# The roots of three norms by two reciprocals and one product, and the last half row of the output scaled and stored in two pieces

## The chip, the cores and the metric

The kernel runs on one core of a Trainium2 chip, as one program. The metric is the device time of one execution in microseconds (us). Before the change three runs gave 902.17, 900.99 and 902.10 us, with a median of 902.1. The five engines are named as in the profile: TensorE is PE (its weight loads PEld), VectorE is DVE, ScalarE is ACT, GpSimd is POOL, and SyncE (SP) issues most DMAs.

## The reference

One layer (DEPTH is 1) on 1024 tokens of 1024 channels, in float32. The norms are what the change touches: the first and the last have one root for each token, `layernorm` has one too.

```python
def rmsnorm(x, g):
    xf = x.astype(jnp.float32)
    y = xf * lax.rsqrt(jnp.mean(xf * xf, axis=-1, keepdims=True) + EPS)
    return (y * g.astype(jnp.float32)).astype(x.dtype)
...
        h = rmsnorm(x, norm_g[l])
        proj = h @ w_in[l]
        q, k, v, za, u, vs, zs, gm = jnp.split(proj, IN_SPLITS, axis=-1)
        ...
        a = window_sink_attention(q, k, v, att_sinks[l])
        a = (a * jax.nn.silu(za)) @ w_att_out[l]
        sgo = chunked_spatial_gating(jax.nn.gelu(u, approximate=False),
                                     jax.nn.gelu(vs, approximate=False),
                                     sg_w[l], sg_b[l], sg_ln_g[l], sg_ln_b[l])
        sgo = (sgo * jax.nn.silu(zs)) @ w_sg_out[l]
        ga, gs = jnp.split(jax.nn.sigmoid(gm + b_merge[l]), N_BRANCHES, axis=-1)
        y = ga * a + gs * sgo
        x = x + y @ w_o[l]
    return rmsnorm(x, final_g)
```

`chunked_spatial_gating` begins with `layernorm(v, ln_g, ln_b)`, whose root is that of the variance plus EPS (1e-6).

## The kernel before, in words

All large products are made on TensorE by a scheme of seven products for eight: a pair of 512-column halves of an input and of a weight is summed and subtracted into forms (`b11`, `t1`, `t2`, `b21`, `t3`, `b22`, `t4`), and each float32 operand is split into a high part in a rounded format (`wh`, or a form's `h`) and the low rest (`wl`, or a form's `l`). A product is then three matmuls for each 128 rows: high by high, high by low, low by high. ScalarE makes the high part by a cast or copy, VectorE the low part by a subtraction (`split`, lines 164 and 165; `form_of`, lines 642 and 643).

At the start, the eight tiles of `x` (128 tokens each) are loaded, and `scale_of(t)` squares and sums a tile on ScalarE (line 614) and calls `rstd_of`. `turned_half` scales each half of the tile by the root and the gain on VectorE (line 624), and TensorE transposes it, four blocks of 128 x 128 into a `ps_sc` bank (line 629). `form_of` makes `T_b11h`, `T_b21h` on ScalarE and `T_b11l`, `T_b21l` on VectorE out of these banks, and ScalarE copies the banks out for later sums (lines 656 and 658). The first large product starts at once behind, `first_product` (its matmuls are line 750, its copy line 773), tile by tile, between the transposes. Its weights come from HBM and are split by `split_vs` (line 727 makes a `wl` on VectorE). Ahead of all this TensorE runs matmuls on ones (line 554).

`rstd_of` computes one over the root of the mean plus epsilon. Before the change ScalarE makes the root `rt`, VectorE its reciprocal `r0`, and one Newton step in full follows, r0 * (1.5 - 0.5 * ve * r0 * r0), with `ve` the mean plus epsilon on VectorE: five VectorE instructions for one column (lines 137, 141, 144, 151, 152), six for eight columns. With `times_minus_2` the last root of the program ends one instruction earlier (line 146): it is then -2 times the wanted value, and the gains of that row are multiplied by -0.5 ahead of time (`g_last`, line 1942).

At the end, the output projection runs in four pairs of token tiles (`for p in range(4)`). Each quarter of a pair is added to `x` (line 1904), squared and summed on ScalarE (line 1906), and when both halves of a row tile are there, `rstd_of` is called (the first half's sum gives the base). `scale_and_store` scales by root and gain and stores. For the first three pairs this happens inside the next pair, with the stores on the POOL queue. For the last pair (p = 3) two quarters are multiplied by the gain on GpSimd ahead of the root (line 1910) and then by the root on ScalarE (line 1924), the other two are scaled on VectorE (line 1930); the last product is made in two pieces of 256 columns (line 1993), and its sum of squares too (line 1995).

The kernel does not write the engines' order by hand: a scheduler places the instructions of each engine's queue, with its own estimate of times, within the data's order and some order-only links (`after`). Engines run their queues in order and wait for each other by semaphores. The small tiles `st` come from a rotation of 16 buffers, those of eight columns from one of 5.

Of the kernel before, what the change touches and what calls it, by code (L numbers as in the profile page):

```python
# [30 lines left out]
P = 128  # L31
# [21 lines left out]
def hybrid_tile(  # L53
# [52 lines left out]
    nc.gpsimd.memset(eps_sb[:], EPS)  # L106
# [27 lines left out]
    def rstd_of(ss, scale, base=EPS, n=1, times_minus_2=False):  # L134

        ve = mtile([P, n], F32, f"st{n}", 16 if n == 1 else 5)
        of_mean.append(nc.vector.tensor_scalar(ve[:], ss, scale, base, op0=ALU.mult, op1=ALU.add))
        rt = mtile([P, n], F32, f"st{n}", 16 if n == 1 else 5)
        of_root.append(nc.scalar.activation(rt[:], ss, AF.Sqrt, bias=eps_sb[:] if base is EPS else base, scale=scale))
# [3 lines left out]
        if n == 1:  # L143
            nc.vector.scalar_tensor_tensor(e[:], ve[:], r0[:], r0[:], op0=ALU.mult, op1=ALU.mult)
            if times_minus_2:
                nc.vector.scalar_tensor_tensor(e[:], e[:], 3.0, r0[:], op0=ALU.subtract, op1=ALU.mult)
                return e
        else:
            nc.vector.tensor_mul(e[:], ve[:], r0[:])
            nc.vector.tensor_mul(e[:], e[:], r0[:])  # L150
        nc.vector.tensor_scalar(e[:], e[:], -0.5, 1.5, op0=ALU.mult, op1=ALU.add)
        nc.vector.tensor_mul(e[:], e[:], r0[:])
# [92 lines left out]
    def half_of(half):  # L245
        return slice(half * HALF, (half + 1) * HALF)
# [1635 lines left out]
    g_out, g_last = g_both[:, 0:2, :], g_both[:, 2:4, :]  # L1882
# [8 lines left out]
    for p in range(4):  # L1891
# [10 lines left out]
        def add_and_square(i, half, src, sign):  # L1902
# [4 lines left out]
            if p == 3 and i == half:  # L1907
                scaled[i, half] = mtile([P, HALF], F32, gtag(), 1, pool)
                gain = (g_last if i else g_out)[:, half, :]
                nc.gpsimd.tensor_tensor(scaled[i, half][:], z, gain, op=ALU.mult)  # L1910
            if i in sq:
                sq[i] = rstd_of(ss[:], 1.0 / D, sq[i][:])
            else:
                nc.vector.tensor_scalar(ss[:], ss[:], 1.0 / D, EPS, op0=ALU.mult, op1=ALU.add)
                sq[i] = ss

        def scale_and_store(i, p=p, t=t, xr=xr, sq=sq, scaled=scaled):
            r = sq[i]
            row = slice((t + i) * P, (t + i + 1) * P)
            for e in range(2):  # L1920
# [8 lines left out]
                gain = (g_last if p == 3 and i else g_out)[:, e, :]  # L1929
                by_gain = nc.vector.scalar_tensor_tensor(z, z, r[:], gain, op0=ALU.mult, op1=ALU.mult)  # L1930
                if p < 3 or i == 0:

                    after(by_gain, pace[0])
# [6 lines left out]
        copied = nc.scalar.copy(x12[:], acc)  # L1940
        if p == 2:
            after(nc.scalar.mul(g_last, g_out, -0.5), copied)
# [45 lines left out]
        for e in range(2):  # L1988
# [7 lines left out]
            if e == 0:  # L1996
                base = mtile([P, 1], F32, "st1", 16)
                nc.vector.scalar_tensor_tensor(base[:], ss[:], 1.0 / D, sq[1][:], op0=ALU.mult, op1=ALU.add)
            else:
                sq[1] = rstd_of(ss[:], 1.0 / D, base[:], times_minus_2=True)  # L2000
# [85 lines left out]
```

## Time and profile before

| | |
|---|---|
| runs | 902.17, 900.99, 902.10 us |
| the profiled execution | 900.83 us, span 899.0 us |
| PE busy | 890.0 us (99%) |
| DVE busy | 683.5 us (76%) |
| ACT busy | 529.5 us (59%) |
| POOL busy | 153.6 us (17%) |
| granted clock of TensorE | 0.998 (mean) |
| HBM | 147.74 MB read, 86.11 MB written |

The span is the time from the first to the last instruction of the profiled execution; the execution's own time is 1.8 us longer. Rows of the order of time give the start in us from the span's start, the duration in us, the engine, the line, the operation, and out<-in by tile names. "x2" behind a row means that two instructions are merged in it, with the duration from the first one's start to the last one's end. What stands in brackets is the idle time ahead of it and what ended that.

### The profile page before, as it was taken

Reading aid. Unit: us, or ns where it says so; the run is one execution under the profiler, and the core shown is the slowest. Engines: PE = TensorE matmul, PEld = TensorE weight load, DVE = VectorE, ACT = ScalarE, POOL = GpSimd, SP = SyncE. Lnnn points to the kernel's source line nnn. Section 1 sums busy time; section 2 is a strip of 40 time slices with the busy share of each in tenths; the row PEclk is TensorE's granted clock in tenths of the full one; section 3 lists DMA queues with packets and bytes.
Section 4 is the critical chain, followed back from the end, with each engine's and each line's share of the span. In section 5 each row is a group of like instructions: output and inputs, shape, how many; then the busy total and the mean of one; then the engine's idle time right before and its main releaser. Section 6 shows DMA issues by size and latency. Waiting matters only on the chain.

```text
span 899.0 us, 13239 instructions
## 1 busy us (share of the span) xinstructions
PE 890.0 (99%) x4306; PEld 745.2 (83%) x4306; DVE 683.5 (76%) x1248; ACT 529.5 (59%) x1062; POOL 153.6 (17%) x218
## 2 busy tenths in 40 slices
PE   9999999999999999999999999999999999999997
PEld 6888888888888888888888888888888888888885
DVE  7859966666687788888878888647797488479986
ACT  7866533334445567677777776755585376467453
POOL 4322222203030001111210111101121121110012
PEclk9999999999999999999999999999999999999999
DMA  9997888858778767878786789899899789998533
GB/s 331 216 270 205 267 204 174 167 156 263 254 252 281 216 191 213 217 149 209 186 219 227 250 240 202 221 333 361 297 293 370 288 227 258 305 294 287 185 116 119
DMA packets 132750, 213.77 MB, mean 238 GB/s; under 512 B 12777, under 2 KB 61161, under 8 KB 132682
## 3 DMA queue, kind: packets, MB, share of 16 engines
q1 hardware_dynamic: 110072, 149.74, 50.0%
q0 software_dynamic: 22464, 62.93, 31.4%
q8 instruction: 34, 0.56, 0.2%
q14 instruction: 34, 0.28, 0.1%
q10 hardware_dynamic: 146, 0.27, 0.1%
HBM read 147.74 MB, written 86.11 MB: 260 GB/s over the span
## 4 chain that ended last, share of the span: by engine, by line
PE 98%; DVE 1%; ACT 0%; issue 0%; DVEq 0%
PE ps_mm L355 42%; PE ps_o L355 27%; PE ps_tp L355 7%; PE ps_sc L1344 3%; PE ps_sc L355 3%; PE ps_tp L750 2%; PE ps_o L1431 2%; PE ps_o L750 2%; PE ps_tp L1390 2%; PE ps_mm L750 2%; PE ps_tp L1015 2%; PE ps_sc L750 1%; PE ps_sc L629 1%; PE ps_sc L554 1%; DVE wl L727 0%
## 5 line engine op out<-in xcount | busy, mean ns | idle before, releaser
L164 ACT CAST wh<-s 128x1024 fp32r<-128x1024 f32 (+1 forms) x79 | 79.3, 1005 | 91.8 <-PE ps_mm L355 42.0
L165 DVE TENSOR_TENSOR wl<-wr,wh 128x512 fp32r<-128x512 f32 (+1 forms) x77 | 72.0, 937 | 54.1 <-ACT wh L164 53.4
L165 DVE TENSOR_TENSOR wl<-s,wh 128x1024 fp32r<-128x1024 f32 (+1 forms) x79 | 92.9, 1176 | 10.5 <-ACT wh L164 10.4
L164 ACT CAST wh<-wr 128x512 fp32r<-128x512 f32 (+1 forms) x77 | 63.0, 820 | 59.1 <-PE ps_mm L355 30.8
L355 PE MATMUL ps_o<-T_t1h,wh 128*128 128x512 f32 x148 | 58.6, 396 | 0.0
L355 PE MATMUL ps_o<-T_t1h,wl 128*128 128x512 f32 x148 | 57.7, 390 | 0.0
L355 PE MATMUL ps_o<-T_t1l,wh 128*128 128x512 f32 x148 | 57.6, 389 | 0.0
L1359 ACT ACTIVATE pr<-ps_sc,sm 128x192 f32<-128x192 f32 (+2 forms) x128 | 50.9, 410 | 8.3 <-DVE sm L1353 7.3
L355 PE MATMUL ps_mm<-T_t3h,wh 128*128 128x512 f32 x140 | 54.9, 392 | 0.0
L355 PE MATMUL ps_mm<-T_b11h,wh 128*128 128x512 f32 x140 | 54.9, 392 | 0.0
L355 PE MATMUL ps_mm<-T_b11l,wh 128*128 128x512 f32 x140 | 54.7, 391 | 0.0
L355 PE MATMUL ps_mm<-T_t3h,wl 128*128 128x512 f32 x140 | 54.6, 390 | 0.0
L355 PE MATMUL ps_mm<-T_b11h,wl 128*128 128x512 f32 x140 | 54.6, 390 | 0.0
L355 PE MATMUL ps_mm<-T_t2h,wl 128*128 128x512 f32 x140 | 54.6, 390 | 0.0
L355 PE MATMUL ps_mm<-T_t2h,wh 128*128 128x512 f32 x140 | 54.6, 390 | 0.0
L355 PE MATMUL ps_mm<-T_t2l,wh 128*128 128x512 f32 x140 | 54.6, 390 | 0.0
L355 PE MATMUL ps_mm<-T_t3l,wh 128*128 128x512 f32 x140 | 54.5, 389 | 0.0
L355 PE MATMUL ps_mm<-T_t4h,wh 128*128 128x512 f32 x136 | 53.5, 393 | 0.0
L355 PE MATMUL ps_mm<-T_t4h,wl 128*128 128x512 f32 x136 | 53.2, 391 | 0.0
L355 PE MATMUL ps_mm<-T_t4l,wh 128*128 128x512 f32 x136 | 53.0, 389 | 0.0
L309 POOL DMA_DIRECT2D sums<-in_w_dram x40 | 29.4, 930 | 91.8 <-ACT x L373 42.7
L355 PE MATMUL ps_o<-T_b22h,wh 128*128 128x512 f32 x108 | 42.7, 395 | 0.0
(420 smaller groups left out, 2452.0 us busy)
## 6 DMA issues: line engine op xcount, KB each, us to landing
wr<-in_w_dram SPq DMA_DIRECT2D x86, 256.0 KB
sums<-in_w_dram POOLq DMA_DIRECT2D x20, 512.0 KB, 6.5
s<-sums SPq DMA_DIRECT2D x20, 512.0 KB
q_hl<-qhl SPq DMA_DIRECT2D x16, 512.0 KB
q<-q_hl SPq DMA_DIRECT2D x64, 128.0 KB
y_dr<-x POOLq DMA_DIRECT2D x28, 256.0 KB, 7.1
g<-in_w_dram POOLq DMA_DIRECT2D x12, 512.0 KB, 6.5
wr<-in_w_dram SPq DMA_DIRECT2D x11, 512.0 KB
```

Source lines behind the costliest of these rows:

```text
L164: hi_of.append(nc.scalar.copy(hi, src))
L165: return nc.vector.tensor_sub(lo, src, hi.bitcast(F32))
L309: return lambda: paced(nc.gpsimd.dma_start(dst, src, accum_op=op))
L355: nc.tensor.matmul(acc, lt, rt, start=fresh and k == 0 and n == 0, stop=k == 3 and n == 2, skip_group_check=True,)
L554: feed(nc.tensor.matmul(idle[:], ones_r[:, 0:P], ones_r, start=True, stop=True))
L629: turns.append(nc.tensor.transpose(pt[:, i * P : (i + 1) * P], xt[:, k * P : (k + 1) * P], ident[:]))
L750: mm = nc.tensor.matmul(acc[:], lt, rt, start=fresh and k == 0 and n == 0, stop=k == 3 and n == terms[-1], skip_group_check=True,)
L1015: nc.tensor.matmul(pm[:, t * P : (t + 1) * P], xh[:, half * 4 + t, g * P : (g + 1) * P], bias[-1][1][:, g % 4, :], start=True, stop=True,)
L1344: nc.tensor.matmul(sc[:, i, k0:], q_of[:, c, i * P : (i + 1) * P], kt[:, f, k0:], start=f == 0, stop=f == 1,)
L1359: nc.scalar.activation(held_in[c, i], sc[:, i, lo:hi], AF.Exp, bias=nmax[:, c, i : i + 1], scale=-1.0, accum_out=sums[:, c, i : i + 1],)
L1390: nc.tensor.transpose(dst, pr[:, i, block * P : block * P + width], ident[:])
L1431: nc.tensor.matmul(po[:, cs], lt, rt, start=n == 0, stop=n == len(terms) - 1)
```

## The change

`rstd_of` works with four times the mean plus epsilon in all places. ScalarE's root is then twice the wanted one, rt = 2 * sqrt(m). VectorE takes the reciprocal of `ve` = 4 * m (`rv`), and of `rt` (`r0`), and the result is rt * rv + r0, which is again one Newton step. For one column this is one instruction on VectorE, so that a root has four there and not five. The eight-column form has a product and a sum. The sums that go into a root get the factor 4 where they are made. `times_minus_2`, the gains times -0.5 and ScalarE's instruction for them are gone. The last half row is scaled on VectorE in two pieces of 256 columns, and each is stored by a DMA of its own on the SP queue.

```diff
-    nc.gpsimd.memset(eps_sb[:], EPS)
+    nc.gpsimd.memset(eps_sb[:], 4.0 * EPS)
...
-    def rstd_of(ss, scale, base=EPS, n=1, times_minus_2=False):
+    def rstd_of(ss, scale, base=4.0 * EPS, n=1):
         ve = mtile([P, n], F32, f"st{n}", 16 if n == 1 else 5)
-        of_mean.append(nc.vector.tensor_scalar(ve[:], ss, scale, base, op0=ALU.mult, op1=ALU.add))
+        of_mean.append(nc.vector.tensor_scalar(ve[:], ss, 4.0 * scale, base, op0=ALU.mult, op1=ALU.add))
         rt = mtile([P, n], F32, f"st{n}", 16 if n == 1 else 5)
-        of_root.append(nc.scalar.activation(rt[:], ss, AF.Sqrt, bias=eps_sb[:] if base is EPS else base, scale=scale))
+        rv = mtile([P, n], F32, f"st{n}", 16 if n == 1 else 5)
+        nc.vector.reciprocal(rv[:], ve[:])
+        bias = base if not isinstance(base, float) else eps_sb[:]
+        of_root.append(nc.scalar.activation(rt[:], ss, AF.Sqrt, bias=bias, scale=4.0 * scale))
         r0 = mtile([P, n], F32, f"st{n}", 16 if n == 1 else 5)
         nc.vector.reciprocal(r0[:], rt[:])
         e = mtile([P, n], F32, f"st{n}", 16 if n == 1 else 5)
         if n == 1:
-            nc.vector.scalar_tensor_tensor(e[:], ve[:], r0[:], r0[:], op0=ALU.mult, op1=ALU.mult)
-            if times_minus_2:
-                nc.vector.scalar_tensor_tensor(e[:], e[:], 3.0, r0[:], op0=ALU.subtract, op1=ALU.mult)
-                return e
+            nc.vector.scalar_tensor_tensor(e[:], rt[:], rv[:], r0[:], op0=ALU.mult, op1=ALU.add)
         else:
-            nc.vector.tensor_mul(e[:], ve[:], r0[:])
-            nc.vector.tensor_mul(e[:], e[:], r0[:])
-        nc.vector.tensor_scalar(e[:], e[:], -0.5, 1.5, op0=ALU.mult, op1=ALU.add)
-        nc.vector.tensor_mul(e[:], e[:], r0[:])
+            nc.vector.tensor_mul(e[:], rt[:], rv[:])
+            nc.vector.tensor_add(e[:], e[:], r0[:])
         return e
...
-                gain = (g_last if p == 3 and i else g_out)[:, e, :]
+                gain = g_out[:, e, :]
+                if p == 3 and i:
+                    for c in range(2):
+                        cs = slice(c * HALF // 2, (c + 1) * HALF // 2)
+                        nc.vector.scalar_tensor_tensor(
+                            z[:, cs], z[:, cs], r[:], gain[:, cs], op0=ALU.mult, op1=ALU.mult
+                        )
+                        nc.sync.dma_start(out[row, half_of(e)][:, cs], z[:, cs])
+                    continue
...
-        copied = nc.scalar.copy(x12[:], acc)
-        if p == 2:
-            after(nc.scalar.mul(g_last, g_out, -0.5), copied)
+        nc.scalar.copy(x12[:], acc)
...
-                nc.vector.scalar_tensor_tensor(base[:], ss[:], 1.0 / D, sq[1][:], op0=ALU.mult, op1=ALU.add)
+                nc.vector.scalar_tensor_tensor(base[:], ss[:], 4.0 / D, sq[1][:], op0=ALU.mult, op1=ALU.add)
             else:
-                sq[1] = rstd_of(ss[:], 1.0 / D, base[:], times_minus_2=True)
+                sq[1] = rstd_of(ss[:], 1.0 / D, base[:])
```

Since the scheduler places the instructions by its own times, the queues change beyond these lines. Behind `rstd_of` the new file's line numbers are one smaller than before (L727 becomes L726), and in the tail four or more larger. The queue of VectorE at the second tile of `x` stood so before (`st1_34` is the root, `wr_27` the tile, `wl_46` and `s_48` low parts of weights):

```order
L137 TENSOR_SCALAR st1_31_184<-st1_30_182 128x1
L141 RECIPROCAL st1_33_188<-st1_32_186 128x1
L144 SCALAR_TENSOR_TENSOR st1_34_190<-st1_31_184,st1_33_188 128x1
L151 TENSOR_SCALAR st1_34_190<-st1_34_190 128x1
L643 TENSOR_TENSOR T_b21l_14_152<-ps_sc_36_203,T_b21h_13_151 128x4x128
L152 TENSOR_TENSOR st1_34_190<-st1_34_190,st1_33_188 128x1
L727 TENSOR_TENSOR wl_46_233<-T_t3l_26_171,wh_45_232 128x1024
L165 TENSOR_TENSOR s_48_238<-T_t3l_26_171,s_47_237 128x1024
L624 SCALAR_TENSOR_TENSOR wr_27_174<-wr_27_174,st1_34_190,ps_tp_9_125 128x512
L624 SCALAR_TENSOR_TENSOR wr_27_174<-wr_27_174,st1_34_190,ps_tp_10_126 128x512
```

and stands so now, on the same engine at the same place (`wr_28` is the tile, `wl_48` and `s_50` the low parts):

```order
L138 TENSOR_SCALAR st1_32_184<-st1_31_182 128x1
L141 RECIPROCAL st1_34_187<-st1_32_184 128x1
L145 RECIPROCAL st1_35_190<-st1_33_186 128x1
L148 SCALAR_TENSOR_TENSOR st1_36_192<-st1_33_186,st1_34_187,st1_35_190 128x1
L623 SCALAR_TENSOR_TENSOR wr_28_174<-wr_28_174,st1_36_192,ps_tp_10_126 128x512
L642 TENSOR_TENSOR T_b21l_14_152<-ps_sc_38_203,T_b21h_13_151 128x4x128
L726 TENSOR_TENSOR wl_48_233<-T_t3l_27_171,wh_47_232 128x1024
L164 TENSOR_TENSOR s_50_238<-T_t3l_27_171,s_49_237 128x1024
L623 SCALAR_TENSOR_TENSOR wr_28_174<-wr_28_174,st1_36_192,ps_tp_9_125 128x512
```

One of the two scalings of the tile now stands ahead of `T_b21l` and the two low parts of weights, and the root's end no longer has `T_b21l` between its steps. On TensorE some groups of transposes stand elsewhere between the matmuls of the first products. The queue of ScalarE between the second and the third tile stood so before:

```order
L656 ACTIVATE xh_4_119<-ps_sc_36_203 128x512
L614 ACTIVATE wT_15_153,st1_51_267<-wr_39_217 128x1024
L773 COPY xh_4_119<-ps_o_59_298 128x512
L642 CAST T_b11h_11_149<-ps_sc_49_250 128x4x128
L139 ACTIVATE st1_53_271<-st1_51_267,eps_sb_72 128x1
```

and stands so now:

```order
L613 ACTIVATE wT_15_153,st1_53_267<-wr_41_217 128x1024
L655 ACTIVATE xh_4_119<-ps_sc_38_203 128x512
L772 COPY xh_4_119<-ps_o_62_298 128x512
L143 ACTIVATE st1_55_271<-st1_53_267,eps_sb_72 128x1
L641 CAST T_b11h_11_149<-ps_sc_51_250 128x4x128
```

The third tile's square root has moved from behind the cast of `T_b11h` to ahead of it. The end of VectorE's queue, behind the last sums of the output, stood so before (`st1_1616` and `st1_1627` are the last two roots):

```order
L1998 SCALAR_TENSOR_TENSOR st1_1620_8886<-st1_1618_8883,st1_1606_8832 128x1
L1993 TENSOR_TENSOR bq0_1600_8760<-bq0_1600_8760,ps_sc_1621_8888 128x256
L1930 SCALAR_TENSOR_TENSOR bq0_1600_8760<-bq0_1600_8760,st1_1616_8864,bq3_1513_8308 128x512
L137 TENSOR_SCALAR st1_1624_8905<-st1_1622_8902,st1_1620_8886 128x1
L141 RECIPROCAL st1_1626_8909<-st1_1625_8907 128x1
L144 SCALAR_TENSOR_TENSOR st1_1627_8911<-st1_1624_8905,st1_1626_8909 128x1
L146 SCALAR_TENSOR_TENSOR st1_1627_8911<-st1_1627_8911,st1_1626_8909 128x1
L1930 SCALAR_TENSOR_TENSOR bq0_1600_8760<-bq0_1600_8760,st1_1627_8911,bq3_1513_8308 128x512
```

and stands so now (`st1_1632` and `st1_1644` are the roots):

```order
L1997 TENSOR_TENSOR bq0_1615_8759<-bq0_1615_8759,ps_sc_1637_8887 128x256
L2002 SCALAR_TENSOR_TENSOR st1_1636_8885<-st1_1634_8882,st1_1621_8831 128x1
L1937 SCALAR_TENSOR_TENSOR bq0_1615_8759<-bq0_1615_8759,st1_1632_8865,bq3_1522_8308 128x512
L138 TENSOR_SCALAR st1_1640_8904<-st1_1638_8901,st1_1636_8885 128x1
L141 RECIPROCAL st1_1642_8907<-st1_1640_8904 128x1
L145 RECIPROCAL st1_1643_8910<-st1_1641_8906 128x1
L148 SCALAR_TENSOR_TENSOR st1_1644_8912<-st1_1641_8906,st1_1642_8907,st1_1643_8910 128x1
L1932 SCALAR_TENSOR_TENSOR bq0_1615_8759<-bq0_1615_8759,st1_1644_8912,bq3_1522_8308 128x256 x2
```

The small instruction that makes `base` (line 1998, now 2002) has moved from ahead of the last sum to behind it; four steps now lead from the last sum of squares to the last scaling as before, and that scaling is two instructions.

9 lines of the change are left out of this document (4 added, 5 removed).

## The prediction

> **What bounds the kernel now.** I read the page first, then who waited for whom on TensorE alone, then busy time by stretch, and last the order of time on each engine in the two places where TensorE is not busy. The page gives the span and TensorE's share:
>
> ```profile
> span 899.0 us, 13239 instructions
> PE 890.0 (99%) x4306; PEld 745.2 (83%) x4306; DVE 683.5 (76%) x1248; ACT 529.5 (59%) x1062; POOL 153.6 (17%) x218
> ```
>
> The view of waits, asked for TensorE over the whole program, has three lines:
>
> ```profile
> PE ps_sc L554 <- DVE T_b22l L103: 1.5, 1, 1.5
> PE ps_o L750 <- DVE wl L727: 0.4, 1, 0.4
> PE ps_mm L750 <- ACT T_b11h L642: 0.2, 1, 0.2
> ```
>
> The second of them is the one at 13.96 us below; the others lie before it. Busy time by stretch (the columns are PE, PEld, DVE, ACT, POOL, clock, DMA share, GB/s) says the same of what follows:
>
> ```profile
> 55.00:850.00 795.00, 795.00 (x3867) 668.23 (x3866) 599.68 (x1060) 467.70 (x936) 123.58 (x175) 1.00 0.84 243
> 850.00:892.44 42.44, 42.44 (x199) 35.45 (x197) 36.48 (x87) 19.48 (x47) 9.43 (x14) 1.00 0.31 113
> ```
>
> From 55 us to the last matmul's end at 892.44 TensorE is never idle. So the end can move in two ways only: through what TensorE loses in the first 55 us, since everything behind moves by as much, and through the 6.56 us behind the last matmul.
>
> **The change part by part: what is covered.** A root of one column had five VectorE instructions (mean plus epsilon, reciprocal, product, line, product) and now has four. The second reciprocal hangs on the mean alone; the first product of before hung on the reciprocal of the root. Eight roots belong to the eight tiles of x at the start, one (of eight columns) to the layer norm, six to the first three pairs of output tiles, two to the last pair. The layer norm's and the six lie behind 55 us and before the last matmul, and are covered by TensorE's unbroken 795.00 of 795.00 and 42.44 of 42.44 us; so is ScalarE's product of the gains with -0.5, which goes. Without that cover they would be worth some 0.2 us a root. I take nothing.
>
> **The start.** The shorter root is the smaller part of what happens here: the order on VectorE changes with it. These are VectorE's rows for the second tile of x, before:
>
> ```profile
> 11.35 0.15 DVE L137 TENSOR_SCALAR st<-st 128x1 f32<-128x1 f32 x1
> 11.41 0.15 DVE L141 RECIPROCAL st<-st 128x1 f32<-128x1 f32 x1
> 11.60 0.32 DVE L144 SCALAR_TENSOR_TENSOR st<-st,st 128x1 f32<-128x1 f32 x1
> 11.95 0.15 DVE L151 TENSOR_SCALAR st<-st 128x1 f32<-128x1 f32 x1
> 12.02 0.68 DVE L643 TENSOR_TENSOR T_b21l<-ps_sc,T_b21h 128x512 fp32r<-128x512 f32 x1
> 12.62 0.15 DVE L152 TENSOR_TENSOR st<-st,st 128x1 f32<-128x1 f32 x1
> 12.68 1.22 DVE L727 TENSOR_TENSOR wl<-T_t3l,wh 128x1024 fp32r<-128x1024 f32 x1
> 13.82 1.22 DVE L165 TENSOR_TENSOR s<-T_t3l,s 128x1024 fp32r<-128x1024 f32 x1
> 14.95 1.40 DVE L624 SCALAR_TENSOR_TENSOR wr<-wr,st,ps_tp 128x512 f32<-128x512 f32 x2
> ```
>
> and these TensorE's, which reads `T_b21l` at 12.96 and `wl` at 13.96:
>
> ```profile
> 12.96 0.63 PE L750 MATMUL ps_o<-wh,T_b21l 128*128 128x512 f32 x2
> 13.96 0.73 PE L750 MATMUL ps_o<-wl,T_b21h 128*128 128x512 f32 x2 [0.37 <-DVE wl L727]
> 15.96 1.18 PE L629 MATMUL ps_sc<-ident,wr 128*128 128x128 f32 x8
> 17.26 0.73 PE L750 MATMUL ps_mm<-wh,T_b11h 128*128 128x512 f32 x2
> 17.83 0.62 PE L750 MATMUL ps_mm<-wl,T_b11h 128*128 128x512 f32 x2
> 18.29 0.63 PE L750 MATMUL ps_mm<-wh,T_b11l 128*128 128x512 f32 x2
> ```
>
> In the new order one half of the tile is scaled right behind the root, ahead of `T_b21l` and `wl`. Step by step from 11.35: the second reciprocal follows its mean by some 0.19 (as the step that hangs on a reciprocal does, 11.41 to 11.60), 11.54; the other reciprocal, which hangs on nothing new, 0.06 later (11.35 to 11.41), 11.60; the product 0.19 later, 11.79; the half scaled 0.25 later, 12.04; `T_b21l` 0.66 behind that (of two scalings in 1.40, one lasting 0.75, the second starts 0.65 behind the first), 12.70; `wl` 0.60 behind (12.02 to 12.62), 13.30 instead of 12.68. So `wl` is 0.62 us later. TensorE waited for just this instruction, so its matmuls at 13.96 begin at 14.58. **+0.62 us.** The two small steps taken out have saved about 0.1 of the 0.66 put in.
>
> The next wait is ScalarE's:
>
> ```profile
> 16.11 0.59 ACT L773 COPY xh<-ps_o 128x512 f32<-128x512 f32 x1 [1.40 <-PE ps_o L750]
> 16.62 0.59 ACT L642 CAST T_b11h<-ps_sc 128x512 fp32r<-128x512 f32 x1
> 17.10 0.30 ACT L139 ACTIVATE st<-st,eps_sb 128x1 f32<-128x1 f32 x1
> 17.30 0.58 ACT L642 CAST T_b21h<-ps_sc 128x512 fp32r<-128x512 f32 x1
> ```
>
> TensorE's group at 17.26 starts when the cast of `T_b11h` (16.62 plus 0.59) ends. Now the third tile's square root stands ahead of that cast and not behind it, and takes 0.20 (17.10 to 17.30): **+0.20 us**, 0.82 in all, 18.08 for that group. Behind it, VectorE makes this tile's `T_b11l` only behind the third root and half a scaling: root on ScalarE at 17.24, first reciprocal 0.33 later (893.47 to 893.80 below: ScalarE's root and the reciprocal that waits for it), product 17.76, half scaled 18.01, `T_b11l` 18.67 to 19.36. But TensorE's new order puts two products of `T_b21h` ahead of those with `T_b11l`; they and the two pairs before them take 0.57 (17.26 to 17.83), 0.46 (17.83 to 18.29) and 0.46, and TensorE asks for `T_b11l` at 19.57. It is there 0.2 us before. So this second delay is hidden, barely.
>
> From there to 55 us I have no single row. Transposes of later tiles go earlier between the matmuls and meet ScalarE's copies out of the same two banks; I have no price for one such meeting but the 0.20 above. I take +0.3, between nothing (TensorE always has other matmuls in hand) and 1.3 (two further half scalings of 0.66 fall on the path). The start: +1.1 us.
>
> **The tail.** VectorE, ScalarE and the stores behind the last matmul:
>
> ```profile
> 892.48 0.42 DVE L1993 TENSOR_TENSOR bq<-bq,ps_sc 128x256 f32<-128x256 f32 x1
> 892.82 0.74 DVE L1930 SCALAR_TENSOR_TENSOR bq<-bq,st,bq 128x512 f32<-128x512 f32 x1
> 893.48 0.21 DVE L137 TENSOR_SCALAR st<-st,st 128x1 f32<-128x1 f32 x1
> 893.80 0.16 DVE L141 RECIPROCAL st<-st 128x1 f32<-128x1 f32 x1
> 894.00 0.22 DVE L144 SCALAR_TENSOR_TENSOR st<-st,st 128x1 f32<-128x1 f32 x1
> 894.25 0.16 DVE L146 SCALAR_TENSOR_TENSOR st<-st,st 128x1 f32<-128x1 f32 x1
> 894.45 0.75 DVE L1930 SCALAR_TENSOR_TENSOR bq<-bq,st,bq 128x512 f32<-128x512 f32 x1
> ```
> ```profile
> 893.47 0.29 ACT L139 ACTIVATE st<-st,st 128x1 f32<-128x1 f32 x1
> 893.67 1.49 ACT L1924 ACTIVATE g<-g,st 128x512 f32<-128x512 f32 x2
> 895.20 0.40 ACTq L1927 DMA_DIRECT2D out_dram<-g  x1
> 895.23 0.33 SPq L1934 DMA_DIRECT2D out_dram<-bq  x1
> ```
>
> The last root had its short form already (three steps behind ScalarE's root), so little is won. The small step that makes `base` now stands behind the second sum of 892.48 and pushes the scaling to 892.89 and the mean to 893.55; its reciprocal 0.24 later, 893.79 (a step with two tensors is answered in 0.25, 894.00 to 894.25); the root's reciprocal 893.86; the product 894.05; scaling from 894.30 and not 894.45: -0.15. The two pieces: 256 columns take 0.34 to the next instruction (892.48 to 892.82) and 0.42 to the end, so the first piece goes out at about 894.75 and the second at 895.10, not all of it at 895.23. ScalarE's half is still held by its first product (893.67 plus about 0.74), so its store goes out at 895.16, not 895.20. What the stores gain from this is less, since they share the DMA engines; from 894 us on, in slices of 0.1 us, those are busy thus:
>
> ```profile
> DMA  0000589999943899999648999999999999500000
> ```
>
> There is little between the four stores to fill: about 0.1 us at 896.0. The bounds are -0.5 (the 0.15 of the root and half of a transfer of about 0.7 us, four of them in the 2.9 us of that row) and +0.7 (a store in twice as many packets could take twice as long). I take -0.1, nearest to the row of the engines' busy share.
>
> By the Trainium skill, "DMA: Bandwidth & Descriptors", section "Anatomy of one DMA", a DMA costs about 2.0 us whatever its size plus its bytes over 436 GB/s; an estimate from this is 2.3 us for the half piece and 2.6 for the whole, so with the 0.13 of the later issue the sum's tail would be -0.4 and not -0.1. The trace's 256 KB stores on the POOL queue took 2.4 us, near that:
>
> ```profile
> out_dram<-bq POOLq DMA_DIRECT2D x12, 256.0 KB, 2.4
> ```
>
> but the last two stores here run side by side, which that formula does not hold.
>
> **The sum.** +0.62 +0.20 +0.3 -0.1 = +1.0 us. The profiled execution took 900.83 us with a span of 899.0; it would take 901.8. It lies 1.3 below the median of the three runs, 902.1 (900.99 to 902.17), so for the median I say 903.1 us, a ratio of 1.001. About 0.2% (1.8 us) is what a measurement of this kernel can tell from no change.
>
> **The rivals.** *Slower for certain:* the 0.2 us by which `T_b11l` arrives in time is not there, and the half scalings stand in TensorE's way in the third and fourth tile too. Each costs 0.66 behind its point (`T_b11l` later than 19.57 in the reckoning above); with two of them 1.0 + 1.3 = +2.3, and 904.4 us. For it: VectorE is the engine that TensorE waits for at 13.96, and four tiles have the new order. Against: TensorE's rows were moved to suit.
>
> *The parts cancel:* the later stretch costs nothing, the tail gives its full 0.5, and ScalarE's 0.20 is absorbed: +0.62 - 0.5 = +0.1, 902.2 us. For it: ScalarE sat 1.40 us idle ahead of 16.11.
>
> *Faster for certain:* the shorter roots let the start's waits vanish (0.37 and 0.24) and the copy-to-cast step of 0.5 with them, and the tail gives 0.15 for the root, 0.33 for the half scaling and 0.35 for half a transfer: -1.9, 900.2 us. Against: the order of rows shows the scaling ahead of `wl`, which adds to the first wait.
>
> *The clock:* TensorE's new waits could lower its clock. Its first five matmuls stood 0.46 us apart, in the trace's row
>
> ```profile
> 1.45 2.50 PE L554 MATMUL ps_sc<-T_b22l 128*128 128x512 f32 x5 [1.45 <-DVE T_b22l L103]
> ```
>
> where later matmuls stand 0.23 apart (two in 0.46). A second such stretch of ten matmuls would cost 2.3: 1.0 + 2.3 = +3.3, 905.4 us. The wait of 0.37 at 13.96 had no such effect, and the granted clock is 1.00 in every stretch up to 892 us. The Trainium skill, "TensorE: Matmul & The Clock Gate", section "A second HAM failure mode: psum-queue depth-cycling", tells of short idle times between groups of matmuls that made the clock swing; by that rule this rival decides, and the trace so far does not bear it out.
>
> **How the numbers follow.** Forecast 0.50, cancelling 0.11, slower for certain 0.29, clock 0.04, faster for certain 0.06. Slower by over 0.2% is 0.33, within 0.2% 0.61, faster 0.06. The range goes from 901.3 (start only +0.2, tail -0.5, and 0.5 for the runs' own scatter) to 905.2 (the slower rival with 0.8 more, from the upper bound of the stores or a third scaling); the clock and the faster case are outside.
>
> **What would show it.** In the new trace: `wl` of line 726 starts at about 13.3 and TensorE's matmuls with it at 14.6; its group on `T_b11h` starts at about 18.1; TensorE is busy without a gap from 55 us on, and its last matmul ends about 1.1 us later, at 893.5; behind it lie about 6.4 us. If the last matmul ends where it did, the start's terms are wrong; if it ends over 2 us later, a further scaling fell on the path; if what lies behind it shrinks by over 0.3, the split of the store is worth more than I say.

## The result, and the profile after

The changed kernel took 906.01 us (median of 6, 905.05 to 909.17), the kernel before 901.4 us (median of 6). The ratio is 1.0056, with a 95% interval of 1.0045 to 1.0068: slower by 4.6 us by the medians and 5.0 by the ratio, where I forecast +1.0 and gave 905.2 as the upper end. Two later series of the same kernel gave 906.89 (903.10 to 909.74) and 906.79 us (903.28 to 909.52). Its 18 runs spread over six us, and those of before mostly over two. The profiled execution is the longest of its six, 909.17 us.

The page of the changed kernel, span and TensorE's share:

```profile
span 907.4 us, 13222 instructions
PE 893.9 (99%) x4306; PEld 747.6 (82%) x4306; DVE 681.8 (75%) x1233; ACT 528.5 (58%) x1061; POOL 153.5 (17%) x218
```

There are 17 instructions fewer, and VectorE is busy for 1.7 us less; the span is 8.4 us longer. The view of TensorE's waits has eight lines where it had three (us in total, times, longest us). Six of them:

```profile
PE ps_mm L749 <- ACT wh L163: 1.6, 1, 1.6
...
PE ps_sc L628 <- issue: 1.4, 1, 1.4
PE ps_mm L749 <- ACT T_b11h L641: 0.6, 2, 0.4
PE ps_mm L749 <- DVE wl L164: 0.5, 1, 0.5
PE ps_o L749 <- DVE wl L726: 0.4, 1, 0.4
PE ps_o L749 <- DVE T_b21l L642: 0.3, 1, 0.3
```

The first two shown, of over 1 us each, are new, and neither is in the first 20 us, where I had looked. A table of when TensorE starts the same group in three profiles shows where they fall (starts of the rows in the order of time, us; the last column is the start of its last row plus 0.28):

| group of TensorE | before | after | after, second profile |
|---|---|---|---|
| `wl` by `T_b21h` (second tile) | 13.96 | 14.76 | 14.46 |
| first `T_b11h` of the next tile | 17.26 | 18.20 | 17.92 |
| first product of `T_t2h`, `T_t1h` | 38.15 | 38.48 | 38.22 |
| the same into `ps_sc` | 51.16 | 55.09 | 53.58 |
| first `wh` by `T_t2h` | 62.03 | 65.97 | 64.46 |
| first `wh` by `T_t3h` | 72.92 | 81.21 | 75.34 |
| last matmul's end | 892.44 | 900.56 | 894.50 |

The lag of 0.94 at 18 us is down to 0.33 at 38 us; a part of it was work that merely stands elsewhere in the new order. Between 38 and 55 us come 3.6 us, and in the first profile 4.4 more between 66 and 81. From there to the last matmul little changes. (The second profile is of an execution of 903.10 us, the shortest of its series; a third, `again2` below, is of 909.52, the longest of its own. No run near the median was profiled, so what a run of 906 us is made of is not shown.)

**The first wait, near 43 us.** Rows of ScalarE in the order of time after the change, from the square of the seventh tile (t = 6) to its root:

```profile
33.22 1.07 ACT L613 ACTIVATE wT<-wr 128x1024 f32<-128x1024 f32 x1
...
36.65 1.05 ACT L645 CAST wh<-T_t3l 128x1024 fp32r<-128x1024 f32 x1 [1.04 <-DMA T_t3l<-T_t3h]
...
39.94 1.05 ACT L645 CAST wh<-T_t3l 128x1024 fp32r<-128x1024 f32 x1 [0.75 <-DMA T_t3l<-T_t3h]
40.89 0.57 ACT L772 COPY xh<-ps_o 128x512 f32<-128x512 f32 x1
41.37 0.29 ACT L143 ACTIVATE st<-st,eps_sb 128x1 f32<-128x1 f32 x1
```

The sum of squares is there at 34.4. Its square root stands behind two casts of a weight (`s4`, raw in `T_t3l`) that wait for an accumulating DMA, and comes at 41.37. In the kernel before it stood ahead of them:

```profile
35.42 0.29 ACT L139 ACTIVATE st<-st,eps_sb 128x1 f32<-128x1 f32 x1
...
39.63 2.03 ACT L646 CAST wh<-T_t3l 128x1024 fp32r<-128x1024 f32 x2
```

On VectorE the root's end and the two scalings follow the second low part of that weight, and TensorE's transposes follow the scalings:

```profile
41.02 1.23 DVE L646 TENSOR_TENSOR wl<-T_t3l,wh 128x1024 fp32r<-128x1024 f32 x1 [0.67 <-ACT wh L645]
42.16 0.15 DVE L145 RECIPROCAL st<-st 128x1 f32<-128x1 f32 x1
42.35 0.22 DVE L148 SCALAR_TENSOR_TENSOR st<-st,st,st 128x1 f32<-128x1 f32 x1
42.60 1.41 DVE L623 SCALAR_TENSOR_TENSOR wr<-wr,st,xh 128x512 f32<-128x512 f32 x2
```
```profile
43.46 1.33 PE L628 MATMUL ps_sc<-ident,wr 128*128 128x128 f32 x8 [1.44 <-issue]
```

**The second wait, near 73 us.** ScalarE's copy at 69.26 waits 4.9 us for an accumulating DMA, `xh<-xh`. It needs none of that DMA's data: its own come from TensorE's bank `ps_sc`, but it overwrites the half tile that the DMA adds from (`raw_t2` and `keep_t5` in the kernel). The cast of the next weight stands behind it in ScalarE's queue, and TensorE runs out of weights:

```profile
69.26 0.59 ACT L787 COPY xh<-ps_sc 128x512 f32<-128x512 f32 x1 [4.89 <-DMA xh<-xh]
...
72.11 1.03 ACT L163 CAST wh<-T_t3h 128x1024 fp32r<-128x1024 f32 x1
```
```profile
73.19 0.73 PE L749 MATMUL ps_mm<-wh,T_t2h 128*128 128x512 f32 x2 [1.61 <-ACT wh L163]
74.45 0.73 PE L749 MATMUL ps_mm<-wl,T_t2h 128*128 128x512 f32 x2 [0.53 <-DVE wl L164]
```

Before, the first of the two sums was issued at 49.93, and the same copy started at 61.91:

```profile
49.93 1.56 POOL L601 DMA_DIRECT2D xh<-xh  x1
```
```profile
61.91 0.59 ACT L788 COPY xh<-ps_sc 128x512 f32<-128x512 f32 x1 [1.48 <-DMA xh<-xh]
```

GpSimd's queue shows that the two sums into `xh` are now issued at 53.19 and 55.47, and not at 49.93 and 54.94, since the eighth tile's sum into `x` stands ahead of the first of them and waits for ScalarE:

```profile
52.65 0.86 POOL L600 DMA_DIRECT2D x<-T_t4l  x1 [2.00 <-ACT T_t4l L673]
53.19 1.21 POOL L600 DMA_DIRECT2D xh<-xh  x1
55.47 0.86 POOL L600 DMA_DIRECT2D xh<-xh  x1 [1.08 <-DVE xh L677]
```

So of the 7.35 us by which the copy is later, 3.26 lie ahead of the sum's issue and 4.09 behind it.

**The clock.** Behind each of the two waits TensorE's clock falls to half for 3.41 us, which I put at half of that, 1.7 us, each time. By stretch (length, TensorE's busy time with its matmuls, clock, DMA share, GB/s):

```profile
41.40:44.81 3.41, 1.77 (x10) 1.00 1.04 161
44.81:48.22 3.41, 3.41 (x9) 0.50 1.03 362
48.22:51.63 3.41, 3.41 (x20) 1.00 0.75 266
72.12:75.53 3.41, 1.81 (x7) 1.00 0.50 154
75.53:78.94 3.41, 3.41 (x10) 0.50 0.06 22
```

**The end.** Last matmul, scaling and stores:

```profile
900.28 0.28 PE L354 MATMUL ps_sc<-T_t4h,wl 128*128 128x256 f32 x1
```
```profile
902.42 0.88 DVE L1932 SCALAR_TENSOR_TENSOR bq<-bq,st,bq 128x256 f32<-128x256 f32 x2
```
```profile
902.97 0.91 SPq L1935 DMA_DIRECT2D out_dram<-bq  x2
```

The scaling begins 1.86 us behind the last matmul's end, where it began 2.01 behind it before (894.45 less 892.44). The span ends 6.84 us behind it, where it ended 6.56 behind it.

### The profile page after: what moved, and what is told of

The parts are those of the page before. It is cut to its first block, busy times and chain, and to the rows that moved or that the text cites. A ratio compares the mean times of both kernels' runs of the same rounds, so it can differ in the third digit from the quotient of the medians.

```text
span 907.4 us, 13222 instructions
## 1 busy us (share of the span) xinstructions
PE 893.9 (99%) x4306; PEld 747.6 (82%) x4306; DVE 681.8 (75%) x1233; ACT 528.5 (58%) x1061; POOL 153.5 (17%) x218
## 4 chain that ended last, share of the span: by engine, by line
PE 95%; DMA 2%; DVE 1%; issue 1%; ACT 0%; POOL 0%; DVEq 0%; ACTq 0%; POOLq 0%
PE ps_mm L354 42%; PE ps_o L354 27%; PE ps_tp L354 7%; PE ps_sc L1343 3%; PE ps_sc L354 3%; PE ps_o L1430 2%; PE ps_tp L1389 2%; PE ps_tp L749 2%; PE ps_mm L749 2%; DMA xh<-xh 2%; PE ps_tp L1014 2%; PE ps_o L749 1%; DMA T_t4h<-in_w_dram 1%; PE ps_sc L553 1%; PE ps_sc L628 0%
```

## The experiments

Every kernel was timed beside the kernel before on the same chip, in 5 rounds. The medians of before were 901.15, 901.09, 901.15 and 900.77 us in the four groups.

**Which part of the change.** Two kernels split it. In both, `newton` selects the five-instruction form, with the factor 4 left in (its line is then 3 - x instead of 1.5 - 0.5 x).

```diff
-        return xt, rstd_of(ss[:], 1.0 / D)
+        return xt, rstd_of(ss[:], 1.0 / D, newton=True)
```

> The changed kernel, but the eight roots of x at the start go back to the Newton step of five VectorE instructions (in the scale of 4); TensorE's order is then that of before, word for word, and the layer norm, the middle roots, the last roots and the two stores stay as in the change. Theory of the start (the loss of some 4.6 us is made in the first 55 us, by the new order that the short root brings there): back to 901.4 plus 0.3 for the end, 901.7 us, ratio 0.999 to 1.001. Rival (the loss is in the short roots of the middle, in the end, or in a transfer behind 55 us): 904 to 906 us, ratio above 1.003.

Measured: 900.78 us, ratio 0.9995 (0.9983 to 1.0008). TensorE's waits are those of before: 0.5 us on `wl`, 0.2 on `T_b11h`, and none behind 20 us in the view. The other half, with `newton=True` everywhere else, the gains' constant and the whole store put back:

> The other half: short roots for the eight tiles of x alone; the layer norm, the middle and the last roots by Newton steps, the gains of the last row times a constant on ScalarE and the last half row scaled and stored whole, as before (in the scale of 4). TensorE's order is that of the changed kernel, word for word. Theory of the start: all of the loss but the 0.3 of the end, 905.7 us, ratio 1.004 to 1.006, with the idle time of TensorE at 42 to 43.5 us and the low clock behind it in the profile. Rival (middle and end): 901 to 902.5 us.

Measured: 908.57 us, ratio 1.0082 (1.0068 to 1.0095), with waits of 1.4 us near 43 and 1.7 and 0.5 near 73, and both stretches of low clock. It is longer than I expected from its part, and its four runs lie within the spread of the changed kernel. So all of the loss comes with the roots at the start; the middle and the end lose nothing that this measure can tell.

**The root or the order.** The roots at the start bring both a shorter form and another order of four queues. Two kernels take them apart. Each instruction that the start issues on TensorE, VectorE, ScalarE and GpSimd is noted as it is made, and order-only links tie each queue to a table (shortened here). Such instructions all show the line of the noting helper in a profile, L798 or L811.

```diff
+    placed = {
+        "tensor": (
+            0, 1, 2, 3, 4, 5, 6, 7, 24, 25, 26, 27, 28, 29, 30, 31, 32, 33, 34, 35, 36, 37, 38, 39,
...
+    }
+    for engine, places in placed.items():
+        seen = start_nc.all[engine].seen
+        for one, two in zip(places, places[1:]):
+            after(seen[two], seen[one])
```

> The changed kernel, with the queues of TensorE, ScalarE, VectorE and GpSimd over the start (all that is issued for the eight tiles of x and the first products) tied by order-only links to the order that they had before; each short root's second reciprocal stands right behind its mean, its last product where the Newton step began. Theory of the order (the short root costs nothing, the order that the scheduler makes with it does): 901.4 less up to 0.3 at the start and 0.3 more at the end, 901.2 to 901.7 us, no idle time of TensorE behind 20 us. Rival (the short root itself is late, by its two reciprocals or its more st buffers): 904 us or more.

> The converse: the eight roots at the start by the Newton step as before, the four queues tied to the order of the changed kernel; everything behind the start as in the change. Theory of the order: the loss is all there although no short root is left at the start, 905.5 to 909 us, with TensorE idle near 43 and near 73 us. Rival (short root itself): 901.5 to 902.5 us.

Measured: the short roots in the order of before 901.65 us, ratio 1.0012 (0.9996 to 1.0028), with no wait from 20 to 200 us and two that I had not expected, of 0.74 at 234.31 and 0.85 at 317.86; the Newton step in the new order 906.88 us, ratio 1.0061 (1.0048 to 1.0074). The second one's waits have no short root at the start behind them:

```profile
PE ps_mm L762 <- ACT wh L811: 1.8, 1, 1.8
...
PE ps_sc L811 <- issue: 1.4, 2, 1.2
```

By the medians the arithmetic costs nothing that this measure can tell, and the order that the scheduler made with it costs the 5 us. One thing is left open: four of the 11 runs in the order of before took 903.57 to 905.94 us, where the kernel beside it took over 903.5 in one run of 21. None of the four was profiled.

**The first wait.** Which instruction of the order? The first try moved the seventh tile's root alone; the scheduler placed the rest anew:

```diff
+    for c in range(2):
+        after(hi_s4[c], of_root[6])
```

> The changed kernel with one order-only link more: the two casts of a weight on ScalarE that wait for an accumulating DMA stand behind the square root of the seventh tile of x, not ahead of it. Theory of the seventh root (TensorE waits 1.4 us at 43.46 for that tile's transposes because its root stood behind those casts, and the clock falls to half for 3.4 us behind it): the idle time at 42 to 43.5 goes, the clock stays at 1.00 from 40 to 55 us, and of the loss about 1.2 from the first 20 us and 0.3 at the end are left: 902.5 to 903.0 us. Rival (the tile is late because everything in the first 20 us is late, the root's place is only a sign of it): 905.5 to 906 us, TensorE's idle time of over 1 us stays somewhere in 40 to 50 us.

Measured: 906.77 us, ratio 1.0060 (1.0046 to 1.0073); the theory's number did not come. VectorE shows why, with the two halves of the scaling around the low parts:

```profile
38.27 0.75 DVE L623 SCALAR_TENSOR_TENSOR wr<-wr,st,xh 128x512 f32<-128x512 f32 x1
38.94 1.22 DVE L647 TENSOR_TENSOR wl<-T_t3l,wh 128x1024 fp32r<-128x1024 f32 x1
41.14 1.23 DVE L647 TENSOR_TENSOR wl<-T_t3l,wh 128x1024 fp32r<-128x1024 f32 x1 [0.98 <-ACT wh L645]
42.29 0.74 DVE L623 SCALAR_TENSOR_TENSOR wr<-wr,st,xh 128x512 f32<-128x512 f32 x1
```

The root was early, but half of the tile was still scaled behind a low part whose cast waits for the DMA. TensorE waited 1.03 us for it. So the next kernel ties the changed kernel's own order and moves the root and both scalings. On VectorE (tile numbers shortened):

```
+RECIPROCAL st1_112<-st1_110
+SCALAR_TENSOR_TENSOR st1_113<-st1_110,st1_111,st1_112
+SCALAR_TENSOR_TENSOR wr_45<-wr_45,st1_113,xh_4
+SCALAR_TENSOR_TENSOR wr_45<-wr_45,st1_113,xh_4
 TENSOR_TENSOR wl_101<-T_t3l_27,wh_100
 TENSOR_TENSOR T_t1l_82<-xh_4,T_t1h_81
 TENSOR_TENSOR xh_4<-xh_4,T_t4l_85
 TENSOR_TENSOR wl_103<-T_t3l_27,wh_102
-RECIPROCAL st1_112<-st1_110
-SCALAR_TENSOR_TENSOR st1_113<-st1_110,st1_111,st1_112
-SCALAR_TENSOR_TENSOR wr_45<-wr_45,st1_113,xh_4
-SCALAR_TENSOR_TENSOR wr_45<-wr_45,st1_113,xh_4
```

> The changed kernel with its own order tied in all four queues over the start, but for five instructions: the seventh tile's square root stands ahead of both casts of a weight on ScalarE, its last reciprocal, product and two scalings ahead of the first of that weight's two low parts on VectorE. The earlier try moved the root alone and TensorE still waited 1.0 us, since VectorE's second scaling stood behind a low part whose cast waits for an accumulating DMA that lands at 40.0 us. Theory: TensorE's idle time at 42 to 43.5 us goes (under 0.3 left), 1.5 us less than the changed kernel's 906.0, 904.5 us; the second idle time near 73 us stays. Rival (another wait takes its place, as in the earlier try): within 0.5 of 906.0 us.

Measured: 903.10 us, ratio 1.0030 (1.0016 to 1.0045): 2.9 us less than the changed kernel's 906.0. Six of its 11 runs are at 903.10 or below, and one of the changed kernel's 18. In the profile both waits are gone:

```profile
41.70 0.50 PE L798 MATMUL ps_o<-T_t2h,T_t1h 128*128 128x512 f32 x1 [0.34 <-ACT xh L798]
42.03 1.04 PE L798 MATMUL ps_sc<-ident,wr 128*128 128x128 f32 x8
```
```profile
63.61 0.59 ACT L798 COPY xh<-ps_sc 128x512 f32<-128x512 f32 x1 [2.07 <-DMA xh<-xh]
```

I had expected 1.5 of it, and the second wait to stay. It went too in the profiled execution, of 901.91 us: the sums were issued from 51.10 on. That they came earlier because the seventh tile did is argued and not shown, since the changed kernel too can be without the second wait (below). The 11 runs reach up to 909.27.

**The second wait.** Two DMAs exchanged on GpSimd's queue, nothing else:

```
 DMA x<-T_t4l
-DMA x<-T_t4l
 DMA xh<-xh
+DMA x<-T_t4l
 DMA xh<-xh
```

> The changed kernel with two DMAs exchanged on the GpSimd queue and nothing else: the sum into xh for the seventh tile is issued ahead of the eighth tile's sum into x, as before, and not behind it, where it waited for ScalarE's copy T_t4l of the eighth tile. Theory (TensorE's second idle time, near 73 us, 2.1 us, comes from that sum's late landing, for which ScalarE waits 4.9 us with the cast of the next weight behind it): idle time near 73 us down to 0.5 or less, 904.2 us. Rival (the sums are late because the transfers of weights run ahead of them, whatever their order): idle time near 73 us stays, 905.5 to 906.5 us.

Measured: 904.81 us, ratio 1.0045 (1.0033 to 1.0058), 1.2 less than the changed kernel. The runs do not tell that from nothing: these five, 904.15 to 907.13, lie within the changed kernel's 903.10 to 909.74. The sum is issued at 50.64 and not 53.19, and TensorE's wait there falls from 2.1 us to 0.22 and 0.53:

```profile
70.37 0.73 PE L749 MATMUL ps_mm<-wh,T_t2h 128*128 128x512 f32 x2 [0.22 <-ACT wh L798]
```

But the copy still started only at 66.43, 15.8 us behind the sum's issue (16.1 without the edit, 12.0 before). So the place on the queue is at most a part of the delay. The changed kernel itself, profiled again, had the sum done in time without any edit, 11.8 us behind its issue at 51.66:

> The changed kernel itself once more, beside the next ones on the same chip. 905 to 909 us; the profile again with a wait of TensorE of 1.4 us near 43 us and one of 1.6 to 2.1 near 73. If the half clock behind such a wait is not tied to its length (of seven profiles with one, two had low stretches and five had none), this one may have none, and then ends near 906.

```profile
63.48 0.59 ACT L787 COPY xh<-ps_sc 128x512 f32<-128x512 f32 x1 [0.62 <-DMA xh<-xh]
```

There was no second wait, and no low clock: 903.10 us for that execution, 906.89 for the median of six. So neither profile shows that the exchange on the queue shortened the wait. What else holds the sums up? The busy share of the DMA engines from 48 to 56 us, in slices of 0.2 us, in the changed kernel's first profile, is nearly nothing from 51 to 53, although three accumulating DMAs have been issued on GpSimd's queue by then, at 47.49, 48.90 and 49.44:

```profile
DMA  9999999999988321000011113253443642999979
```

Five small loads (two vectors of the layer norm, a bias, the sinks) fall in there: the same view counts 1010 packets under 512 bytes in these 8 us. In the second profile, without the second wait, the same view has no such gap: no slice of these 8 us is below six tenths. The other profiles go with this. The view gives the time from issue to landing of the sums into `xh`, as the median of the two. In the seven profiles with such a gap near 51 to 53 us (`after`, `again2`, `start_only`, `link_t6`, `fill6`, `newton_new_order`, `pool_order`) it is 14.2 to 16.3 us, and in the six without any gap and with the small loads in place 9.2 to 12.6. `start_back` has a shallow one and 12.5, `root7_start` a shallow one from 54 us on and 16.9. The next kernel moved the small loads:

```diff
-    behind(nc.sync.dma_start(lg_sb[:], ln_g), mm)
...
+    mm = by_s4(3)
+    behind(nc.sync.dma_start(lg_sb[:], ln_g), mm)
```

> The changed kernel once more, as the row beside which the next one is read. 903 to 909 us. The first idle time of TensorE near 43 us in the profile (1.4 us and up); the second near 73 only where the sum into xh lands later than some 64 us.

> The changed kernel in its own order, with five small loads of constants (the layer norm's two vectors, the merge bias, the sinks: 4 to 8 bytes in a piece) moved on SyncE's queue from behind the sixth weight load at 45 us to behind four later weight loads, and made to wait for a product at some 66 us. Theory of the small loads (their many tiny packets hold the DMA engines at 50 to 55 us, when those carry little and the sums into x and xh lie still; this makes the second wait): the sum into xh lands before 64 us, no idle time of TensorE near 73 us, 903.5 to 904.5 us and all runs within 2 us. Rival (the sums are late by when they are issued): landing at 66 to 70 in the profile as in most others, time as the changed kernel's within 1 us.

> Short roots, the start in the order of before, the last half row stored whole, and the same five small loads moved. If the small loads cost something in that order too: 900 us or less, fewer runs above 902. Rival (in that order the sums land in time anyway): 900.6 us, as without the move.

Measured: the changed kernel 906.79 us; with the loads moved 905.92, ratio 1.0050 (1.0038 to 1.0062); in the order of before 902.04, ratio 1.0009 (1.0000 to 1.0017), not better than without the move. The DMA engines are busy throughout:

```profile
DMA  9998998999899999999988969699989597989999
```

and the copy starts at 67.32, where it started at 68.68 in the changed kernel of the same group (`again2`); the sums take 14.5 us to land. The four weight loads that stood behind the small ones on SyncE's queue now go out at 48.92 and not at 52.20, ahead of the sums. So moving the small loads does not help. It does not clear them either, since it moved the four weight loads ahead of the sums with them: two things changed at once. In the order of before the same move made a second wait of 0.43 and 0.53 us where there had been none. What sets the landing beside the place on the queue is open; the gap of the DMA engines goes with it, and neither the small loads nor the weight loads were tried alone.

**The start.** My terms of +0.62 and +0.20, undone alone in the changed kernel's order:

> The changed kernel in its own order, but for the first 20 us: the second tile's first half scaling stands behind T_b21l and the two low parts again, the third tile's root behind the cast of T_b11h on ScalarE, and its last reciprocal, product and first scaling behind T_b11l and T_b21l on VectorE. As predicted at first (0.62 and 0.20 on the path, and everything behind moves with it): 0.8 less than the changed kernel. Rival (the wait near 43 us ends with a landing at 40.0 us that doesn't move, so that it only grows by what the start gains): within 0.3 of the changed kernel, with a wait near 43 us of 1.6 to 2.3 us.

Measured: 906.62 us, ratio 1.0056 (1.0035 to 1.0077), and the changed kernel in the same group 906.89. TensorE arrives earlier and waits longer:

```profile
42.01 0.50 PE L798 MATMUL ps_o<-T_t2h,T_t1h 128*128 128x512 f32 x1 [1.05 <-ACT xh L798]
43.95 1.94 PE L798 MATMUL ps_sc<-ident,wr 128*128 128x128 f32 x8 [1.43 <-issue]
```

With runs of 903.27 to 909.46 us the times alone could not tell a gain of 0.8 from none. The profile speaks for the rival: the wait ends with a landing (here the cast at 40.43, 39.94 without the edit) that the start does not bring forward. This profile has no second wait, but one of 1.46 at 239.96 that none of the three of the changed kernel has. With the seventh tile put right as well:

> Both repairs in the changed kernel's order: the seventh tile's root, product and scalings ahead of the low parts that wait, and the first 20 us put back. Theory: the first repair alone gave 903.1; with its wait gone the start's 0.3 to 0.8 counts, 902.3 to 902.8 us. Rival (other waits come up in this order): 903 us or more.

Measured: 903.64 us, ratio 1.0028 (1.0010 to 1.0047), no better than root7 alone. Its ten runs fall in two groups, five of 901.4 to 902.1 and five of 905.2 to 908.7. The profiled one, of 908.67, had a second wait of 3.4 us, for a sum that held the copy until 68.08, and half a clock for 6.83 us.

**The clock.** Six matmuls on data that was there, into the bank that the seventh tile's transposes overwrite:

```diff
+        for _ in range(fill):
+            full = hb["b11"][0]
+            mm = nc.tensor.matmul(pt[:], full[:, 0, 0:P], full[:, 0, :], start=True, stop=True, skip_group_check=True)
```

> The changed kernel with six matmuls more, on data that is there, into the bank that the seventh tile's transposes then overwrite; they stand in TensorE's queue just where it was idle at 42 to 43.5 us. The wait for the scaled tile stays as long as it was. Theory of the clock (of the loss some 2 us are not the wait but the half clock that follows it): TensorE busy through 42 to 43.5, clock 1.00 from 40 to 55 us, 904.0 us. Rival (the wait alone costs, the low clock falls on work that has slack): 906.0 us or a little more, since the filling can last longer than the wait.

Measured: 905.36 us, ratio 1.0046 (1.0033 to 1.0058). The clock stays at 1.00 from 40 to 55 us, but the scheduler also exchanged the two sums on GpSimd's queue, as in pool_order, and TensorE's wait is 0.73 and no longer 1.44. So this run cannot tell what the clock alone was worth. The two profiles of the changed kernel give an estimate: between 38 and 55 us 3.6 us came with waits of 1.60 and the low clock, and 2.4 with waits of 1.89 and full clock, so the clock was worth some 1.5.

**The end.** The short roots, the start in the order of before (the tables of new_old_order), and the last half row whole:

```diff
-                if p == 3 and i:
-                    for c in range(2):
...
+                if p < 3 or i == 0:
+                    after(by_gain, pace[0])
```

> The short roots in all places, the start in the order of before, and the last half row scaled and stored whole by one DMA. Theory of the end (of the 0.22 us that the end has grown, 6.61 to 6.83 us behind the last matmul, the two pieces cost 0.3 to 0.4 and the short root gives 0.15 back): 6.45 us behind the last matmul, 900.9 us, ratio 0.999 to 1.001. Rival (the pieces cost nothing): 6.8 us behind the last matmul.

Measured: 900.58 us, ratio 1.0000 (0.9985 to 1.0016). This is the lowest median of all kernels here, and not to be told from the kernel before.

```profile
span 897.5 us, 13223 instructions
```
```profile
890.85 0.28 PE L354 MATMUL ps_sc<-T_t4h,wl 128*128 128x256 f32 x1
```

The span ends 6.37 us behind the last matmul's end (897.5 less 891.13), before 6.56, after 6.84. So the short root gains 0.19 there and the two pieces cost 0.47. The other profiles agree: 6.78 to 6.88 in the 13 with the short root and two pieces, 6.37 and 6.44 in the two with the short root and one piece, 6.56 and 6.64 in the two with the Newton step and one piece.

## Why the prediction was wrong

**The step that failed** is the sentence "From there to 55 us I have no single row": I took +0.3 there, between nothing and 1.3, for the whole reordering between 20 and 55 us. It was +3.6 us in the first profile and +2.4 in the second (the lag at 55 us less that at 38): waits of 1.60 and 1.89 near 43 us (for ScalarE's copy and for the transposes), and in the first the low clock behind them. I had set the bound by rows of VectorE, two half scalings of 0.66. The true price stood in other rows: a cast that waits for an accumulating DMA, and everything that is queued behind it. The order of ScalarE around the seventh tile's root would have shown the exchange, but I looked only at the first three tiles, where TensorE waited already. My sign for a last matmul over 2 us later, that a further scaling fell on the path, would have named a wrong cause.

**"TensorE is busy without a gap from 55 us on"** failed too, in the executions with the second wait. That wait hangs on a queue that I had not followed, GpSimd's: its sums are issued behind ScalarE's copy of the eighth tile, and then land late, for a reason that stays open.

**The two terms at the start** were met as times of the rows, in part by luck, and wrong in what they are worth. `wl`'s group came 0.80 later, of which 0.17 was there at the first matmuls (9.80 and 9.63), so 0.63 against 0.62; the group of `T_b11h` 0.14 more, against 0.20. But TensorE's idle time up to these two rows grew by 0.35 and 0.60 only (2.06 to 2.41, 2.19 to 2.79); the rest is that the matmuls ahead of them take longer in the new order (15.41 us busy up to the second row, 15.07 before). Then "everything behind moves by as much" failed: at 38 us the lag was 0.33 and the idle time 0.47 more than before, and undoing the terms gained 0.3, which the runs cannot tell from nothing.

**The tail**: the root's -0.15 was right (1.86 against 2.01 behind the last matmul). The split of the store I took as +0.05, within -0.35 and +0.85; it was +0.47. So the tail is +0.28 and not -0.1. The estimate from the Trainium skill, "DMA: Bandwidth & Descriptors", section "Anatomy of one DMA", -0.4, was further off, with the other sign; the fit is given there for DMAs that GpSimd issues, and the last stores here are issued by SyncE and ScalarE.

**The middle** was right at nothing: start_newton has the short roots there and in the layer norm, and lies at 0.9995 (0.9983 to 1.0008).

**The rivals**: "slower for certain" (0.29) had the right sign and the wrong mechanism, further half scalings in the first 20 us. The clock rival (0.04) had half of the mechanism: low clock behind a gap, at 2.3 us each (1.7 by half of the measured 3.41). I gave it little since the wait of 0.37 at 13.96 had brought none, and I did not ask how long a wait must be.

## What to carry to other kernels

Where an edit makes a scheduler set the queues anew, compare the whole queues, not the places where the bound engine waits now: look first for an instruction on the chain to the bound engine that has moved behind one that waits for a DMA, since such a move cost here the rest of the transfer and not the length of the instruction. By the profiles here, a term at the start of a chain counts only as far as the next wait for something that does not move. When a form is better and the time is worse, hold the order fixed and change the form, then the other way round: two kernels told them apart here.

## What the hardware showed that I had not expected

TensorE's low clock comes in stretches of 3.41 us. In the changed kernel's first profile the clock is full for 37.55 us, half for 3.41, full for 27.31, half for 3.41: 11, 1, 8 and 1 times 3.413. If time is cut into windows of that length, on a grid counted from the first switch to full clock in each profile, a low stretch behind 20 us and before the last matmul fills one window, or two in a row, and follows a window in which TensorE was idle for about half. In the 17 profiles there are nine such windows behind 20 us with 1.60 us idle or more: eight were followed by low clock, one (1.74) was not. None of those at full clock with 1.52 or less was. The wait near 43 us is of one length in the changed kernel and in pool_order, 1.44 us, but in the latter the window holds 1.52 us of idle time, since the grid lies otherwise, and the clock stays:

```profile
41.66:45.07 3.41, 1.89 (x11) 1.00 1.06 154
45.07:48.48 3.41, 3.41 (x20) 1.00 0.99 353
```

So one wait costs 1.4 us in one execution and some 3.1 in the next (with the 1.7 of the clock), which goes with much of the spread of 903 to 909.7 us: over the 18 runs of the changed kernel the mean clock is 0.999 in the two shortest (903.10 and 903.28) and 0.994 to 0.995 in the four longest. The Trainium skill, "TensorE: Matmul & The Clock Gate", Part 1, section "What's actually happening", has the window at 3413 ns and free-running, which agrees. How much idle time in a window brings the low clock is read here from the nine windows alone; they do not fix a threshold, and a kernel that sets the length of a wait was not tried.
